# First attention of a two-layer encoder: exponentials divided where they stand, values of the last four heads made later

## The chip, the cores and the metric

The kernel runs on one core of one Trainium2 chip. The core has four engines that matter here, each working through its own instructions strictly in its own order: PE (TensorE, the matrix products, which write into eight banks of accumulator memory), DVE (VectorE), ACT (ScalarE) and POOL (GpSimd); SP starts most DMAs. [...] The metric is the device time of one execution in microseconds.

## The reference

Two encoder layers over 512 tokens of width 1024, in fp32. The first is a latent attention of 8 heads with a block-causal mask, and the change touches only that one:

```python
def block_attn(args):
    qn, qr, blk = args
    s = (jnp.einsum('bqhd,bkhd->bhqk', qn, k_nope) + jnp.einsum('bqhr,bkr->bhqk', qr, k_rope)) * scale
    mask = key_chunk[None, :] <= q_chunk[:, None]
    s = jnp.where(mask[None, None], s, -jnp.inf)
    p = jax.nn.softmax(s, axis=-1).astype(v.dtype)
    return jnp.einsum('bhqk,bkhd->bqhd', p, v)
```

Behind it come the output projection, a gated feed-forward block, a second attention with 16 heads over shared keys and values, and another feed-forward block.

## The kernel before

Every fp32 operand of a matrix product is split in two: a rounded part written by ACT (line 144, tiles whose names end in h or hi) and the rest written by DVE (line 145, names that end in l or lo). `mm3` (lines 355 to 358) then makes three products of them. Tiles are 128 partitions wide.

In the first attention, `Head.scores` handles one tile of 128 queries at a time: five products per tile into a bank `sc`, a DVE instruction that scales, masks and takes the minimum (line 494), an exponential on ACT that also sums its row into one column of `sums` (line 496). `Head.turn` transposes that tile on PE, piece by piece against an identity matrix, into a bank `pt` (line 508) and splits it into `pth` and `ptl`. `pv` multiplies with the values. The rows of the exponentials are not yet divided by their sums at that point: the result, whose columns are queries, has to be multiplied by the inverse sums, and for that each column of `sums` is spread over a bank `bc` by four PE transposes (`spread`, line 469):

```python
            V.reciprocal(sums, sums)
            of = U(name="of")
            nc.scalar.copy(of, o)

            def rest():
                V.tensor_tensor(of, of, spread(sums), op=OP.mult)
                oh, ol = U(F32R, "oh"), U(F32R, "ol")
                split(oh, ol, of)
```

`attention` goes through 32 slots, one for each of the 8 heads' 4 tiles of queries: the scores of a slot, the turn of the tile two slots back, and at the third slot of a head the `pv` of the head before. Between these it takes steps from a filler, a generator that yields after every projection product (`fill_a`). Its order is: values of heads 0 to 3 (`values_a(0)`), the query rotation of heads 0 to 3 (`rotary(0)`), head 0's queries and keys (`heads_a(0)`, 15 products of 512 columns), then `values_a(1)` (24 such products, the values of heads 4 to 7), then heads 1 to 7, with `rotary(1)` ahead of head 4, then the first part of the output projection. Thirteen steps are taken between head 0's projections and its first scores. The weights of all this come through one queue, `feed`, in the order in which they are used: raw tiles by DMA, then `whi` and `wlo` by ACT and DVE, three buffers of each.

The program's text gives priorities; a scheduler fixes the order on each engine ahead of the run. `first(n)` lifts the instructions within it by n places. Banks are handed out from three groups: four of `mm` (projections, `pv`), two of `s` (scores), two of `t` (transposes, `bc`). A projection's bank is free again when both its halves have been read out of it, by ACT and then by DVE.

Of the kernel before, what the change touches and what calls it, by code (L numbers as in the profile page):

```python
# [11 lines left out]
F32R = mybir.dt.float32r  # L12
I32 = mybir.dt.int32
AF = mybir.ActivationFunctionType
OP = mybir.AluOpType
# [3 lines left out]
D, S, P = 1024, 512, 128  # L19
KT = D // P  # L20
CHUNK = 64
H_A, NOPE, ROPE, VD = 8, 128, 64, 128
# [46 lines left out]
def trunk(ctx: ExitStack, tc: tile.TileContext, a, out):  # L69
    nc = tc.nc  # L70
    V = nc.vector
# [10 lines left out]
    def name_(n):  # L82
        uid[0] += 1
        return f"{n}_{uid[0]}"

    def U(dt=F32, name="u"):
        return up.tile([P, S], dt, tag="u", name=name_(name), bufs=NU)
# [4 lines left out]
    def bank(tag="mm", name="b"):  # L92
        return ps.tile([P, S], F32, tag=tag, name=name_(name), bufs={"mm": 4, "s": 2, "t": 2}[tag])

    def small(name="sm"):
        return sp.tile([P, 4], F32, tag="small", name=name_(name))
# [38 lines left out]
    @contextmanager  # L135
    def first(n):

        tc.cur_priority -= n
        yield
        tc.cur_priority += n  # L140


    def split(dst_hi, dst_lo, src):
        return (nc.scalar.copy(dst_hi, src),  # L144
                V.tensor_tensor(dst_lo, src, dst_hi.bitcast(F32), op=OP.subtract))  # L145
# [5 lines left out]
    class Pair:  # L151
# [4 lines left out]
        def __init__(self, src):  # L156
            self.src, self.raw = src, {}
# [191 lines left out]
    feed = Feed()  # L349
# [5 lines left out]
    def mm3(o, l, r, start, stop):  # L355
        nc.tensor.matmul(o, l[0], r[0], start=start, stop=False)  # L356
        nc.tensor.matmul(o, l[0], r[1], start=False, stop=False)  # L357
        nc.tensor.matmul(o, l[1], r[0], start=False, stop=stop)  # L358

    def proj(n_out, n_k, kc, rhs, banks, ahead=True):  # L360

        cols = n_out * P
        for c in range(0, n_k, kc):
            m = min(kc, n_k - c)
            w = feed.next(m * cols, ahead)
            for kk in range(m):
                if kk == 1:
                    feed.ahead()
                while len(rhs) <= c + kk:
                    yield False  # L370
                for j in range(n_out):
                    mm3(banks[j], w(kk * cols + j * P, P), rhs[c + kk], c + kk == 0, c + kk == n_k - 1)
                    yield True
# [9 lines left out]
    def cut(t, c):  # L383
        return t[0][:, c], t[1][:, c]
# [80 lines left out]
    def spread(col, first=0):  # L465

        b = bank("t", "bc")
        for i in range(col.shape[1]):
            nc.tensor.transpose(b[:, (first + i) * P:(first + i + 1) * P],
                                col[:, i:i + 1].to_broadcast([P, P]), ident)  # L470
        return b
# [8 lines left out]
    class Head:  # L480

        def __init__(self, qk, bt, scale, pv, sums):
            self.qk, self.bt, self.scale, self.pv, self.sums = qk, bt, scale, pv, sums
            self.p, self.pt = {}, None

        def scores(self, qt):
            n = P * (qt + 1)
            sc = bank("s", "sc")  # L490
            self.qk(sc[:, :n], qt, n)
            p = U(name="p")
            mn = small("mn")
            V.tensor_tensor_reduce(p[:, :n], sc[:, :n], self.bt(n), scale=self.scale(qt), scalar=3e38,  # L494
                                   op0=OP.add, op1=OP.min, accum_out=mn[:, :1])
            nc.scalar.activation(p[:, :n], p[:, :n], AF.Exp, bias=mn[:, :1], scale=-1.0,  # L496
                                 accum_out=self.sums[:, qt:qt + 1])
            self.p[qt] = p

        def turn(self, qt):  # L500
# [226 lines left out]
        feed.add(a["w_aq"][k], 768)  # L727
    feed.add(a["w_uv"][0], 1024)
    feed.add(a["w_uqr"][0], 768)
    feed.add(a["w_qk"][0], 640)  # L730
    feed.add(a["w_uv"][1], 1024)
    for h in range(1, H_A):
        if h == 4:
            feed.add(a["w_uqr"][1], 768)
        feed.add(a["w_qk"][h], 640)
# [50 lines left out]
    for k in range(KT):  # L786
        h, l = U(F32R, "xh"), U(F32R, "xl")
# [12 lines left out]
    rest = proj(3, KT, 2, xs, b2)  # L800
# [55 lines left out]
    for j in range(2):  # L856
        V.tensor_tensor(ckv[j], ckv[j], rkv, op=OP.mult)
        h, l = U(F32R, "ckh"), U(F32R, "ckl")
# [9 lines left out]
    for j in range(3):  # L868
        h, l = U(F32R, "cqh"), U(F32R, "cql")
        split_scaled(h, l, b2[j], g_q[:, j:j + 1])  # L870
        cqs.append((h, l))
    nsq = consts.tile([P, 4], F32, name="nsq")
# [6 lines left out]
    def A(name):  # L879
        return pool[0].tile([P, S], F32R, tag="a", name=name_(name), bufs=15)  # L880

    va = [pool[0].tile([P, 2, D], F32R, tag="v", name=f"va{tt}", bufs=4) for tt in range(NQT)]
    mask = pool[0].tile([P, S], F32, tag="mask", name="mask", bufs=1)
    nc.gpsimd.memset(mask, 0.0)
    nc.gpsimd.memset(mask[:64, S - 64:], -BIG)
    qr, qk_a, osp = {}, {}, []

    def values_a(c):

        w = feed.next(1024, False)  # L890
        for tt in range(NQT):
            if tt == 1:
                feed.ahead()
            b = bank()
            ts_ = slice(tt * P, (tt + 1) * P)
            for k in range(2):
                mm3(b, cut(cks[k], ts_), w(k * S, S), k == 0, k == 1)
                yield True
            with first(90 if c else 0):
                split(va[tt][:, 0, c * S:(c + 1) * S], va[tt][:, 1, c * S:(c + 1) * S], b)  # L900
# [23 lines left out]
    def heads_a(h):  # L924
        bq = bank()
        w = feed.next(640, False)
        for k in range(3):
            if k == 2:
                feed.ahead()
            mm3(bq, w(k * P, P), cqs[k], k == 0, k == 2)  # L930
            yield True
        qh, ql, kh, kl = (A(n) for n in ("qh", "ql", "kh", "kl"))
        split(qh, ql, bq)
        bk = bank()
        for k in range(2):
            mm3(bk, w((3 + k) * P, P), cks[k], k == 0, k == 1)
            yield True
        split(kh, kl, bk)
        qk_a[h] = qh, ql, kh, kl
        yield h  # L940
# [30 lines left out]
    def query_norm():  # L971
        for j in range(3):
            sq_.add(b2[j])
        rq = rstd_of_scaled(sq_.total(), QL, r0)
        V.tensor_scalar(nsq, rq, -((NOPE + ROPE) ** -0.5), None, op0=OP.mult)

    def rotary_key():

        nc.gpsimd.tensor_tensor(sik[:64], kr[64:], sik[64:], op=OP.mult)
        nc.gpsimd.tensor_tensor(kr[:64], kr[:64], cos[:64], op=OP.mult)  # L980
        nc.gpsimd.tensor_tensor(kr[:64], kr[:64], sik[:64], op=OP.add)
        for e in (LO, HI):
            nc.scalar.copy(kr1[e], kr[:64])
            V.tensor_tensor(kr2[e], kr[:64], kr1[:64].bitcast(F32), op=OP.subtract)

    def fill_a():
        yield from values_a(0)
        query_norm()
        yield from rotary(0)
        rotary_key()  # L990
        yield from heads_a(0)
        yield from values_a(1)
        yield "v"
        for h in range(1, H_A):
            if h == 4:
                yield from rotary(1)
            yield from heads_a(h)
        yield from out_first(osp)

    def start_a(h):  # L1000
        fill.until(h)
        qh, ql, kh, kl = qk_a.pop(h)
        r = qr.pop(h)

        def qk(o, qt, n):
            q_ = slice(qt * P, (qt + 1) * P)
            nc.tensor.matmul(o, qh[:, q_], kh[:, :n], start=True, stop=False)
            nc.tensor.matmul(o, qh[:, q_], kl[:, :n], start=False, stop=False)
            nc.tensor.matmul(o, ql[:, q_], kh[:, :n], start=False, stop=False)
            nc.tensor.matmul(o, r[:, q_], kr1[:, :n], start=False, stop=False)  # L1010
            nc.tensor.matmul(o, r[:, q_], kr2[:, :n], start=False, stop=True)

        def pv(pth, ptl):
            fill.until("v")
            o = bank()
            v_ = slice(h * VD, (h + 1) * VD)
            for kt in range(NQT):
                q_ = slice(kt * P, S)
                mm3(o[:, q_], (va[kt][:, 0, v_], va[kt][:, 1, v_]), (pth[:, kt, q_], ptl[:, kt, q_]),
                    kt == 0, kt == NQT - 1)  # L1020
            V.reciprocal(sums, sums)
            of = U(name="of")
            nc.scalar.copy(of, o)

            def rest():
                V.tensor_tensor(of, of, spread(sums), op=OP.mult)
                oh, ol = U(F32R, "oh"), U(F32R, "ol")
                split(oh, ol, of)
                osp.append((oh, ol))

            return rest

        sums = small("sums")
        return Head(qk, lambda n: mask[:, S - n:], lambda qt: nsq[:, qt:qt + 1], pv, sums)

    firsts = []
    fill = Filler(fill_a())
    attention(H_A, start_a, fill, 13, 8 + 5 * 7 + 6 + 14, False)
    fill.drain()
    st.close()  # L1040
# [462 lines left out]
    rest = v_half(0)  # L1503
# [11 lines left out]
    osp, qk_b, ofs, sums, biases = [], {}, {}, {}, {}  # L1515
# [116 lines left out]
    fill = Filler(fill_b())  # L1632
# [108 lines left out]
```

## Time and profile before

| what | us |
|---|---|
| median of 3 runs | 1124.07 (1122.27 to 1124.4) |
| the profiled execution's own time | 1122.24 |
| its span, first to last instruction | 1120.5 |
| first score product of head 0 | 65.7 from the span's start |
| inverse sums of head 0 and of head 7 taken | 75.2 and 148.3 |

Times within the profile are counted from the start of the span; the execution's own time is 1.7 us longer. A row of the timeline gives the start, the duration, the engine, the line and operation, output and input, shapes, and in square brackets how long the engine had nothing to do before it and what ended that. PEld is the loading of a product's stationary operand.

### The profile page before, as it was taken

The page shows a single profiled execution, that of the slowest core. Times are in us where ns is not written, and L with a number is a line of the kernel's source. Part 1 is how long each engine was busy: PE and PEld are TensorE (multiplying, and loading weights), DVE is VectorE, ACT ScalarE, POOL GpSimd, SP SyncE. Part 2 cuts the span into 40 slices and gives each one's busy share as a digit, 9 for nine tenths or more (in the row PEclk, how much of TensorE's full clock was granted, in tenths as well). Part 3 has the DMA queues.
Part 4 walks back from the last instruction along what each step waited for, and adds up shares of the span by engine and source line. Part 5 has one row for each costly group of instructions (what it writes and reads, how often), then busy time and mean ns, then how long its engine had stood idle before and what let it go on. Part 6 is the DMA issues. An engine that isn't in the chain of part 4 may idle for free.

```text
span 1120.5 us, 18982 instructions
## 1 busy us (share of the span) xinstructions
PE 1104.6 (99%) x6973; PEld 984.4 (88%) x6973; DVE 932.4 (83%) x1671; ACT 685.5 (61%) x1339; POOL 69.1 (6%) x106
## 2 busy tenths in 40 slices
PE   9999999999999999999999999999999999999997
PEld 6788889999999998887788888889999999998885
DVE  6787737999989889978868887758999899889977
ACT  6476636755555556768435767656755555566675
POOL 1200000000000001400000000000000000002402
PEclk9999999999999999999999999999999999999999
DMA  7342216323232358861556565635423322459923
GB/s 234 107 117 67 85 56 227 133 70 107 94 127 95 125 167 241 145 202 29 193 150 168 142 178 148 165 103 181 148 78 95 125 84 95 142 169 289 172 57 76
DMA packets 62990, 150.85 MB, mean 135 GB/s; under 512 B 8432, under 2 KB 10224, under 8 KB 62896
## 3 DMA queue, kind: packets, MB, share of 16 engines
q1 hardware_dynamic: 55552, 136.61, 38.7%
q0 software_dynamic: 6912, 12.59, 6.8%
q8 instruction: 55, 0.90, 0.3%
q10 hardware_dynamic: 432, 0.44, 0.1%
q14 instruction: 39, 0.32, 0.1%
HBM read 119.52 MB, written 9.63 MB: 115 GB/s over the span
## 4 chain that ended last, share of the span: by engine, by line
PE 46%; DVE 3%; DMA 2%; issue 1%; ACT 1%; POOL 0%; SPq 0%; POOLq 0%; DVEq 0%; ACTq 0%
PE al L1446 8%; PE b L356 6%; PE b L357 6%; PE b L358 6%; PE be L1446 4%; PE al L1197 4%; PE be L1197 3%; PE ga L1446 2%; PE pt L508 1%; PE de L1197 1%; PE ga L1197 1%; PE b L1600 1%; PE b L1599 1%; PE sc L1592 1%; PE sc L1591 1%
## 5 line engine op out<-in xcount | busy, mean ns | idle before, releaser
L144 ACT CAST whi<-raw 128x1024 fp32r<-128x1024 f32 (+3 forms) x224 | 225.5, 1007 | 212.6 <-PE al L1446 73.0
L145 DVE TENSOR_TENSOR wlo<-raw,whi 128x1024 fp32r<-128x1024 f32 (+3 forms) x224 | 261.3, 1168 | 57.7 <-ACT whi L144 54.3
L1446 PE MATMUL al<-th,whi 128*128 128x256 f32 x432 | 123.0, 285 | 0.4 <-DVE ut L1458 0.3
L1446 PE MATMUL al<-th,wlo 128*128 128x256 f32 x432 | 121.2, 281 | 0.0
L1446 PE MATMUL al<-tl,whi 128*128 128x256 f32 x432 | 121.0, 280 | 0.0
L356 PE MATMUL b<-xh,whi 128*128 128x512 f32 (+1 forms) x304 | 117.6, 387 | 0.1
L357 PE MATMUL b<-xl,whi 128*128 128x512 f32 (+1 forms) x304 | 113.0, 372 | 0.1
L358 PE MATMUL b<-xh,wlo 128*128 128x512 f32 (+1 forms) x304 | 112.4, 370 | 0.3 <-DVE wlo L145 0.3
L174 DVE TENSOR_TENSOR raw<-raw,raw 128x1024 f32<-128x1024 f32 x72 | 86.7, 1220 | 1.2 <-DMA raw<-in_w_pair 0.9
L1446 PEld LDWEIGHTS al<-th,whi 128*128 128x128 f32 x432 | 81.3, 188 | 2.9 <-DVE ut L1458 0.8
L1446 PEld LDWEIGHTS al<-th,wlo 128*128 128x128 f32 x432 | 81.3, 188 | 0.4 <-DVE wlo L145 0.4
L1446 PEld LDWEIGHTS al<-tl,whi 128*128 128x128 f32 x432 | 81.3, 188 | 0.0
L496 ACT ACTIVATE p<-p,mn 128x128 f32<-128x128 f32 (+1 forms) x96 | 54.0, 563 | 39.5 <-DVE mn L494 38.4
L145 DVE TENSOR_TENSOR ptl<-pt,pth 128x128 fp32r<-128x128 f32 (+1 forms) x96 | 46.7, 487 | 29.4 <-ACT pth L144 23.7
L358 PEld LDWEIGHTS b<-xh,wlo 128*128 128x128 f32 x304 | 57.5, 189 | 10.1 <-DVE wlo L145 0.7
L144 ACT CAST whi<-wd 128x512 fp32r<-128x512 f32 x86 | 49.9, 620 | 26.8 <-PE al L1197 11.9
L145 DVE TENSOR_TENSOR wlo<-wd,whi 128x512 fp32r<-128x512 f32 x86 | 56.5, 689 | 11.5 <-ACT whi L144 11.2
L356 PEld LDWEIGHTS b<-xh,whi 128*128 128x128 f32 x304 | 57.7, 190 | 7.5 <-ACT xh L148 1.0
L357 PEld LDWEIGHTS b<-xl,whi 128*128 128x128 f32 x304 | 57.7, 190 | 7.3 <-DVE xl L149 1.4
L144 ACT CAST pth<-pt 128x128 fp32r<-128x128 f32 (+1 forms) x96 | 40.4, 421 | 26.6 <-PE pt L508 25.6
L1197 PE MATMUL al<-whi,ph 128*128 128x512 f32 x132 | 51.9, 393 | 0.5 <-ACT y L1258 0.5
L1197 PE MATMUL al<-whi,pl 128*128 128x512 f32 x132 | 51.5, 391 | 0.0
(309 smaller groups left out, 3267.4 us busy)
## 6 DMA issues: line engine op xcount, KB each, us to landing
raw<-in_w_pair SPq DMA_DIRECT2D x72, 512.0 KB, 3.6
wd<-in_w_down SPq DMA_DIRECT2D x54, 256.0 KB, 5.6
raw<-in_w_o SPq DMA_DIRECT2D x16, 512.0 KB, 3.5
raw<-in_w_gu SPq DMA_DIRECT2D x16, 512.0 KB, 3.8
raw<-in_w_down SPq DMA_DIRECT2D x16, 512.0 KB, 4.1
raw<-in_w_qkb SPq DMA_DIRECT2D x16, 512.0 KB, 3.5
wd<-in_w_down POOLq DMA_DIRECT2D x22, 256.0 KB, 5.6
wd<-raw POOLq DMA_DIRECT2D x22, 256.0 KB, 4.2
```

The source lines that it names most:

```text
L144: return (nc.scalar.copy(dst_hi, src), V.tensor_tensor(dst_lo, src, dst_hi.bitcast(F32), op=OP.subtract))
L145: V.tensor_tensor(dst_lo, src, dst_hi.bitcast(F32), op=OP.subtract))
L174: V.tensor_tensor(t, x, y, op=OP.add)
L356: nc.tensor.matmul(o, l[0], r[0], start=start, stop=False)
L357: nc.tensor.matmul(o, l[0], r[1], start=False, stop=False)
L358: nc.tensor.matmul(o, l[1], r[0], start=False, stop=stop)
L496: nc.scalar.activation(p[:, :n], p[:, :n], AF.Exp, bias=mn[:, :1], scale=-1.0, accum_out=self.sums[:, qt:qt + 1])
L508: nc.tensor.transpose(t[:, kt * P:(kt + 1) * P], p[:, kt * P:(kt + 1) * P], ident)
L1197: nc.tensor.matmul(to[e], l[c], r[d], start=j < 4 and k == 0 and n == 0, stop=k == NF // 2 - 1 and n == 2, skip_group_check=True)
L1446: nc.tensor.matmul(o, l[c], r[d], start=first_ and n == 0, stop=k == K2 - 1 and n == 2, skip_group_check=True)
L1591: nc.tensor.matmul(o, q1[:, e, q_], k1[:, e, :n], start=True, stop=False)
L1592: nc.tensor.matmul(o, q1[:, e, q_], k2[:, e, :n], start=False, stop=True)
```

## The change

The first attention's heads pass a new flag, `whole`. With it, `scores` divides a tile of exponentials by its sums as soon as they are there: an inverse of one column and a multiplication of the tile by it, both on DVE, both lifted by 20 places. `pv` then splits its bank directly into `oh` and `ol`; the copy `of`, the spreading of the sums and the multiplication with them are gone. In the filler, `values_a(1)` and the mark "v" move from behind head 0 to ahead of head 3, its weights move likewise in `feed`, and only heads 4 to 7 wait for "v".

```diff
+            if self.whole:
+                r = self.sums[:, qt:qt + 1]
+                with first(20):
+                    V.reciprocal(r, r)
+                    V.tensor_scalar(p[:, :n], p[:, :n], r, None, op0=OP.mult)
             self.p[qt] = p
...
-    feed.add(a["w_qk"][0], 640)
-    feed.add(a["w_uv"][1], 1024)
-    for h in range(1, H_A):
+    for h in range(H_A):
+        if h == 3:
+            feed.add(a["w_uv"][1], 1024)
         if h == 4:
...
-        yield from heads_a(0)
-        yield from values_a(1)
-        yield "v"
-        for h in range(1, H_A):
+        for h in range(H_A):
+            if h == 3:
+                yield from values_a(1)
+                yield "v"
             if h == 4:
...
         def pv(pth, ptl):
-            fill.until("v")
+            if h >= 4:
+                fill.until("v")
...
-            V.reciprocal(sums, sums)
-            of = U(name="of")
-            nc.scalar.copy(of, o)
-
-            def rest():
-                V.tensor_tensor(of, of, spread(sums), op=OP.mult)
-                oh, ol = U(F32R, "oh"), U(F32R, "ol")
-                split(oh, ol, of)
-                osp.append((oh, ol))
-
-            return rest
+            oh, ol = U(F32R, "oh"), U(F32R, "ol")
+            split(oh, ol, o)
+            return lambda: osp.append((oh, ol))
...
-        return Head(qk, lambda n: mask[:, S - n:], lambda qt: nsq[:, qt:qt + 1], pv, sums)
+        return Head(qk, lambda n: mask[:, S - n:], lambda qt: nsq[:, qt:qt + 1], pv, sums, True)
```

The line numbers of the changed kernel are 5 higher from line 498 up to `pv`. Three places show how the order on the engines moves. The first is PE behind head 0's projections, whose banks are b_688 (queries) and b_710 (keys). Before, the next rows there were the values (whi_697 here is their weight, ckh the latent keys), each bank of which is read out on its own. The first bank's six rows are shown; the first score product stood 36 rows behind b_710:

```order
L358 MATMUL b_710<-ckh_465,wlo_628 128x512
L356 MATMUL b_720<-whi_697,ckh_460 128x512
L357 MATMUL b_720<-wlo_698,ckh_460 128x512
L358 MATMUL b_720<-whi_697,ckl_461 128x512
L356 MATMUL b_720<-whi_697,ckh_465 128x512
L357 MATMUL b_720<-wlo_698,ckh_465 128x512
L358 MATMUL b_720<-whi_697,ckl_466 128x512
...
L1007 MATMUL sc_788<-kh_706,qh_704 128x128
```

In the changed kernel the same place on PE holds head 1's queries (b_720) and keys (b_742), the first score product after 15 rows, and then head 2's queries (b_751), the fifth bank in a row of a group of four:

```order
L358 MATMUL b_710<-ckh_465,wlo_628 128x512
L356 MATMUL b_720<-cqh_525,whi_697 128x512
...
L358 MATMUL b_742<-ckh_460,wlo_698 128x512
L356 MATMUL b_742<-ckh_465,whi_697 128x512
L357 MATMUL b_742<-ckl_466,whi_697 128x512
L358 MATMUL b_742<-ckh_465,wlo_698 128x512
L1012 MATMUL sc_786<-kh_706,qh_704 128x128
L356 MATMUL b_751<-cqh_525,whi_729 128x512
```

So 21 rows of projections have moved from ahead of the first score product to behind it. The second place is ACT just ahead of the splits of head 0's banks (qh_704 and kh_706). Before, with rh the rotated queries, kr_117 the rotated key, va the values:

```order
L144 CAST whi_771<-raw_695 128x640
L144 CAST rh_648<-ra_643 128x512
L144 CAST va_543<-b_720 128x512
L144 CAST va_544<-b_735 128x512
L144 CAST va_545<-b_744 128x512
L144 CAST rh_657<-ra_652 128x512
L144 CAST qh_704<-b_688 128x512
L144 CAST va_546<-b_753 128x512
L983 CAST kr_117_538<-kr_469 64x512 x2
L144 CAST kh_706<-b_710 128x512
L144 CAST whi_838<-raw_729 128x640
```

and in the changed kernel:

```order
L144 CAST whi_760<-raw_695 128x1024
L144 CAST rh_648<-ra_643 128x512
L144 CAST whi_805<-raw_727 128x640
L144 CAST rh_657<-ra_652 128x512
L988 CAST kr_117_538<-kr_469 64x512 x2
L144 CAST qh_704<-b_688 128x512
L144 CAST kh_706<-b_710 128x512
L144 CAST qh_736<-b_720 128x512
```

Here four casts of values have left, the cast of a further weight (whi_805, head 3's) has come ahead of rh_657, and the key's rotation has come ahead of qh_704. The third place is DVE in the same stretch. Before:

```order
L145 TENSOR_TENSOR wlo_772<-raw_695,whi_771 128x640
L145 TENSOR_TENSOR rl_649<-ra_643,rh_648 128x512
...
L911 TENSOR_TENSOR ra_652<-ra_652,rb_653 128x512
L145 TENSOR_TENSOR va_545<-b_744,va_545 128x512
L145 TENSOR_TENSOR rl_658<-ra_652,rh_657 128x512
L145 TENSOR_TENSOR ql_705<-b_688,qh_704 128x512
L145 TENSOR_TENSOR va_546<-b_753,va_546 128x512
L984 TENSOR_TENSOR kr_118_539<-kr_469,kr_117_538 64x512 x2
L145 TENSOR_TENSOR kl_707<-b_710,kh_706 128x512
```

and in the changed kernel:

```order
L145 TENSOR_TENSOR wlo_761<-raw_695,whi_760 128x1024
L145 TENSOR_TENSOR rl_649<-ra_643,rh_648 128x512
L914 TENSOR_TENSOR ra_652<-b_617,sin_406 128x512
L915 TENSOR_TENSOR rb_653<-b_618,cos_407 128x512
L145 TENSOR_TENSOR wlo_806<-raw_727,whi_805 128x640
L916 TENSOR_TENSOR ra_652<-ra_652,rb_653 128x512
L145 TENSOR_TENSOR rl_658<-ra_652,rh_657 128x512
L989 TENSOR_TENSOR kr_118_539<-kr_469,kr_117_538 64x512 x2
L145 TENSOR_TENSOR ql_705<-b_688,qh_704 128x512
L145 TENSOR_TENSOR kl_707<-b_710,kh_706 128x512
```

The split ql_705, with which head 0's query bank comes free, now stands behind the low half of head 3's weight (wlo_806) and behind both halves of the rotated key. From a place within the output projection on, the order is the same as before on every engine, apart from the numbers.

More of the change, by code (lines that the diff above doesn't have):

```diff
@@ L480, in trunk, with __init__ @@
     class Head:
-        def __init__(self, qk, bt, scale, pv, sums):
-            self.qk, self.bt, self.scale, self.pv, self.sums = qk, bt, scale, pv, sums
+        def __init__(self, qk, bt, scale, pv, sums, whole=False):
+            self.qk, self.bt, self.scale, self.pv, self.sums, self.whole = qk, bt, scale, pv, sums, whole
             self.p, self.pt = {}, None
```

## The prediction

> **What bounds the kernel now.** I read the page first (busy time by engine), then the windows of the first attention, then the list of who waited for whom there.
>
> ```profile
> span 1120.5 us, 18982 instructions
> PE 1104.6 (99%) x6973; PEld 984.4 (88%) x6973; DVE 932.4 (83%) x1671; ACT 685.5 (61%) x1339; POOL 69.1 (6%) x106
> ```
>
> ```profile
> 60.00:80.00 20.00, 19.87 (x107) 16.83 (x106) 17.22 (x38) 15.63 (x35) 0.00 (x0) 1.00 0.48 134
> 80.00:100.00 20.00, 19.77 (x119) 17.08 (x118) 14.06 (x34) 11.49 (x29) 0.00 (x0) 1.00 0.10 30
> 100.00:120.00 20.00, 19.64 (x116) 16.82 (x117) 16.69 (x41) 13.91 (x35) 0.00 (x0) 1.00 0.44 130
> 120.00:140.00 20.00, 20.00 (x121) 17.74 (x120) 14.89 (x35) 13.44 (x34) 0.00 (x0) 1.00 0.16 52
> ```
>
> ```profile
> PEld b L356 <- DVE va L145: 1.1, 2, 0.6
> PEld sc L1007 <- DVE mn L494: 0.8, 2, 0.4
> ```
>
> In a window's row stand its length, then PE, PEld, DVE, ACT and POOL, then the granted clock and the DMA. The reader is to see that PE has something to do nearly all the time, in this stage too, at full clock. The longest waits for others between 58 and 172 us (in the last two rows: total, times, longest) come to no more than a microsecond or so. So a microsecond of PE work removed is worth about a microsecond, and an idle microsecond added to PE costs one: behind it PE is full to the end, and nothing makes it up. DVE has 5.9, 3.3 and 5.1 us free in the three windows from 80 to 140.
>
> **What leaves PE.** Eight heads lose one spreading of the sums each:
>
> ```profile
> 82.12 0.60 PE L469 MATMUL bc<-ident,sums 128*128 128x128 f32 x4
> 82.56 0.38 PE L508 MATMUL pt<-ident,p 128*128 128x128 f32 x2
> 165.09 0.62 PE L469 MATMUL bc<-ident,sums 128*128 128x128 f32 x4
> 165.46 0.36 PE L356 MATMUL b<-oh,whi 128*128 128x256 f32 x1
> ```
>
> Durations overlap, so starts count: 0.44 us of PE for the first, 0.37 for the last. Eight times that is 3.0 to 3.5; I take **3.4 us off**, since most stand within the loop like the first.
>
> **What DVE and ACT gain and lose.** The groups of instructions by line give count, busy time, mean ns of one, and the idle time ahead of them:
>
> ```profile
> L1023 ACT COPY of<-b 128x512 f32<-128x512 f32 x8 | 4.7, 585 | 5.8 <-PE b L358 5.8
> L1026 DVE TENSOR_TENSOR of<-of,bc 128x512 f32<-128x512 f32 x8 | 5.5, 682 | 3.0 <-ACT of L1023 2.6 <-PE bc L469 0.4
> L1021 DVE RECIPROCAL sums<-sums 128x4 f32<-128x4 f32 x8 | 1.4, 176 | 1.2 <-ACT p L496 0.9
> L817 DVE TENSOR_SCALAR rot<-rot,inv 128x128 f32<-128x128 f32 x1 | 0.3, 285 | 0.0
> L1368 DVE TENSOR_SCALAR g<-g 128x512 f32<-128x512 f32 x1 | 0.4, 419 | 0.0
> ```
>
> Per head DVE gets four inverses of one column (no such row; with 0.176 for four columns as a ceiling, 0.7 together) and multiplications of 128, 256, 384 and 512 columns. With 0.285 and 0.419 as their ends and the others between, those are 1.4 us; at the 0.68 of a product with a second tensor per 512 columns they would be at most 1.9. It loses 0.68 + 0.18. So DVE gains 1.2 to 1.7 us a head, and nearly six heads fall into 80 to 140, which had 14.4 us free: 7 to 10 of those would be used. That stays beside PE, at about 90%. It costs nothing while the splits still come in time, and the first places where they may not are below. ACT loses 4.7 us, hidden before and after. The longer chain from a tile's scores to its transposes (some 0.5 us more) lies within the two slots, about 5 us, that PE works in between.
>
> **What the move costs.** Here the order printed ahead of this text decides. In the changed kernel PE does 15 rows behind head 0's banks, and then the first score product needs `kh` of head 0 from ACT, and the next row needs a bank, which only head 0's `ql` on DVE frees: queries and keys of heads 0 and 1 fill all four. Before, 36 rows lay there, with value banks that came free one by one. What the timeline of before says of those two splits, PE first, then ACT, then DVE:
>
> ```profile
> 56.68 0.39 PE L356 MATMUL b<-whi,ckh 128*128 128x512 f32 x1
> 56.91 0.39 PE L357 MATMUL b<-wlo,ckh 128*128 128x512 f32 x1
> 65.69 0.22 PE L1007 MATMUL sc<-kh,qh 128*128 128x128 f32 x1
> ```
>
> ```profile
> 56.70 0.73 ACT L144 CAST whi<-raw 128x640 fp32r<-128x640 f32 x1 [3.16 <-PE b L357]
> 57.33 0.62 ACT L144 CAST rh<-ra 128x512 fp32r<-128x512 f32 x1
> 62.58 0.58 ACT L144 CAST qh<-b 128x512 fp32r<-128x512 f32 x1
> 63.65 1.26 ACT L983 CAST kr<-kr 64x512 fp32r<-64x512 f32 x2
> 64.92 0.59 ACT L144 CAST kh<-b 128x512 fp32r<-128x512 f32 x1
> ```
>
> ```profile
> 57.46 0.83 DVE L145 TENSOR_TENSOR wlo<-raw,whi 128x640 fp32r<-128x640 f32 x1 [0.57 <-ACT whi L144]
> 58.20 0.16 DVE L462 TENSOR_TENSOR r<-r,r 128x4 f32<-128x4 f32 x1
> 62.71 0.69 DVE L145 TENSOR_TENSOR rl<-ra,rh 128x512 fp32r<-128x512 f32 x1
> 63.32 0.69 DVE L145 TENSOR_TENSOR ql<-b,qh 128x512 fp32r<-128x512 f32 x1
> 64.52 1.38 DVE L984 TENSOR_TENSOR kr<-kr,kr 64x512 fp32r<-64x512 f32 x2
> L145 DVE TENSOR_TENSOR wlo<-raw,whi 128x1024 fp32r<-128x1024 f32 x198 | 241.8, 1222 | 49.9 <-ACT whi L144 47.3 <-DMA raw<-in_w_down 2.1
> ```
>
> The row at 56.68 is the first behind b_710, and product follows product every 0.227 us, so the 15 rows end at 56.68 + 3.4 = 60.1. DVE meanwhile, queued behind the inverse root at 58.2: `nsq` to 58.4, the low half of the value weight (1.14 from start to start at this size) to 59.5, `rl`, `ra`, `rb` at 0.60 each to 61.3, the low half of head 3's weight (0.74) to 62.0, the last `ra` with its 0.68 to 62.7. ACT's `rh` can only then run, to 63.4; then `kr` 1.26 to 64.6, `qh` to 65.1, `kh` to 65.6. So the first score product stands at about 65.65 instead of 60.1. DVE's `kr` waits for ACT's and ends at 65.4, `ql` at 66.0, so the next row stands at 66.05. PE is idle for some **5.9 us**. The lower end takes the casts of whi_805 to be all that gates (its buffer is free when row 14 ends, at 60.0): `wlo` to 61.7, `ra` 62.3, `rh` 62.9, `kr` 64.1, `qh` and `kh` 65.2, `ql` 65.6: 5.4. Nothing covers it, as PE takes its rows in order.
>
> Against this, the kernel before reached the first score product at 65.69 with 21 more rows done (21 x 0.227 = 4.8), and its two waits for value splits (1.1 in PEld's row above, 0.6 as pitch) lie within that. The changed one is at the same place 4.5 to 5.0 us later: **4.9 us**.
>
> **Two small waits behind it.** In head 0 DVE has the late `kl` of head 2 and a value split ahead of the fourth tile's line 494 (2 x 0.6, an inverse 0.17, 0.67, the third tile's multiplication 0.35: 2.4 us from the end of the scores), where PE has 2.1 us of rows until it needs that tile. Some 0.5 us is late there, and as much at head 0's `pv`, whose `ptl` now stands behind a weight split. From nothing to 2, I take **1 us**.
>
> **The clock.** The windows and the timeline show no pause of PE of this length, except at the ends:
>
> ```profile
> 1112.60:1116.00 3.40, 0.52 (x3) 0.10 (x1) 2.49 (x6) 0.72 (x2) 1.00 (x1) 1.00 0.21 77
> 1116.00:1120.50 4.50, 0.00 (x0) 0.00 (x0) 1.46 (x3) 0.00 (x0) 0.00 (x0) 0.51 0.49 175
> 1.19 4.02 PE L113 MATMUL warm<-idle 128*128 128x512 bf16 x9 [1.19 <-DVE idle L110]
> 6.69 0.42 PE L358 MATMUL b<-xh,wlo 128*128 128x512 f32 x1
> ```
>
> Some 3 us after the last product the granted clock is at half (0.51), and at the start products of 512 columns stand 0.43 to 0.45 apart (4.02 for nine) until about 6.7, 5.5 us after the first. An idle stretch of 5.9 us is longer than 3, so the clock falls; then PE runs at half for up to 5.5 us, which loses up to half of that, 2.75. I take **1.4 us**, the middle of 0 and 2.75. [...]
>
> **The sum.** -3.4 + 4.9 + 1.0 + 1.4 = +3.9 us on the profiled execution's 1122.24 (1120.5 of span): 1126.1. The median of the runs shown lies 1.8 above that execution, so on it the same sum gives 1128.0. I predict **1127.0**, between the two.
>
> **Rivals.**
> - *The move is harmless* (faster). ACT and DVE reach head 0's splits by 60.1, since four value splits on each (ACT 0.59, DVE 0.60) have left. Then -3.4, and the 0.6 of the value waits goes as well, +1 for the small waits: 1119.2 on the profiled execution. For it: in before, `qh` was ready at 63.2, not 65. Against it: the rotated key, and `rh` behind a weight whose buffer PE frees at 60.0. It decides if `ql` ends before 61.5.
> - *About even.* The idle stretch is there, but no clock loss, no small waits, and the pauses PE makes later in this stage (0.8 for line 494 above) vanish with the relieved banks: -3.4 + 4.9 - 0.8 = +0.7: 1122.9, or 1124.8 on the median.
> - *DVE becomes the bound.* At 90% over heads 1 to 5, with each inverse waiting for ACT, PE waits a further 0.8 us a head: 3.9 + 4 = 1130.1. Against it: DVE's rows sum to less than PE's in each of those heads except that with the second rotation (six more products of 0.6).
>
> That the change does not do what it says is out: the printed order has no line 469 on `sums`, and the values stand behind head 2.
>
> **Chances.** Forecast (+2.3 to +6) 0.50, about even 0.25, DVE the bound 0.13, harmless 0.12. A measurement can tell about 0.2%, 2.25 us. Faster by more: 0.12. Within: the even case and a little of the forecast, 0.27. Slower: 0.61. The range leaves out the harmless case and the far end of DVE's: 1121.5 to 1131. The likeliest case's own is 1124.5 to 1130.
>
> **What would show it.** In the profile after: a pause of PE of 5 to 6 us between 60 and 66, ended by ACT `kh` and DVE `ql`; a granted clock under 1.00 in the windows behind it; no line 469 rows on `sums`; multiplications of 0.2 to 0.45 us; the end of the stage 3 to 5 us later. If PE's first score product comes at 61 or 62, the move is harmless and I am wrong on the whole. If the pause is there and the clock stays at 1.00, the sum is 1.4 less. If DVE's rows between 80 and 120 fill 19 of 20 us and PE waits for `ptl` in each head, it is the third rival.

## The result, and the profile after

| | before | after |
|---|---|---|
| median of 5 runs each | 1122.27 us (1120.22 to 1124.4) | 1130.52 us (1129.52 to 1132.24) |
| ratio, 95% interval | | 1.0079 [1.0066, 1.0091] |
| profiled execution: time, span | 1122.24, 1120.5 | 1132.24, 1130.5 |

The changed kernel is slower by 8 us, where the forecast was 4. The profiled execution of the changed kernel is the slowest of its five, 1.7 us over the median; its span is 10.0 us longer than that of before. The head of its page, and four windows of the first attention (length, then PE, PEld, DVE, ACT and POOL, then the granted clock and the DMA):

```profile
span 1130.5 us, 18959 instructions
PE 1106.1 (98%) x6941; PEld 986.1 (87%) x6941; DVE 940.4 (83%) x1719; ACT 681.4 (60%) x1331; POOL 69.1 (6%) x106
```

```profile
60.00:80.00 20.00, 14.99 (x59) 12.09 (x58) 12.93 (x28) 11.22 (x22) 0.00 (x0) 0.83 0.38 108
80.00:100.00 20.00, 20.00 (x120) 17.71 (x119) 16.65 (x51) 11.93 (x32) 0.00 (x0) 1.00 0.17 54
100.00:120.00 20.00, 17.66 (x96) 14.11 (x95) 17.87 (x43) 11.96 (x27) 0.00 (x0) 0.99 0.38 98
120.00:140.00 20.00, 20.00 (x113) 17.81 (x113) 16.32 (x53) 12.22 (x33) 0.00 (x0) 0.93 0.17 62
```

PE has 32 rows fewer, as it should (6941 for 6973). It is idle in two windows, not in one: 5 us between 60 and 80, and 2.3 between 100 and 120, with a full one in between. The clock falls twice. The list of waits from 56 to 190 us (total, times, longest) has both behind one name, and a smaller one in the output projection, where the first total (`tot`) waits for DVE's sum of squares:

```profile
PEld sc L1012 <- ACT kh L144: 7.3, 2, 5.4
PEld tot L435 <- DVE acc L426: 0.9, 1, 0.9
```

The first pause is the forecast one. In the timeline, PE's last row of head 1's keys starts at 59.84 and the first score product at 65.22; ACT's `kh` and DVE's `ql` of head 0, for which it and the next row wait, start at 64.57 and 64.96:

```profile
59.84 0.39 PE L358 MATMUL b<-ckh,wlo 128*128 128x512 f32 x1
65.22 0.48 PE L1012 MATMUL sc<-kh,qh 128*128 128x128 f32 x1 [4.99 <-ACT kh L144]
65.71 0.80 PE L356 MATMUL b<-cqh,whi 128*128 128x512 f32 x1
```

```profile
64.57 0.59 ACT L144 CAST kh<-b 128x512 fp32r<-128x512 f32 x1
```

```profile
64.96 0.69 DVE L145 TENSOR_TENSOR ql<-b,qh 128x512 fp32r<-128x512 f32 x1
```

The second was not in the forecast's sum. It lies where head 3 ends and head 4 begins. PE first, then ACT:

```profile
114.58 0.48 PE L357 MATMUL b<-ckl,whi 128*128 128x512 f32 x1
114.90 0.40 PE L358 MATMUL b<-ckh,wlo 128*128 128x512 f32 x1
115.54 0.63 PE L513 MATMUL pt<-ident,p 128*128 128x128 f32 x4 [0.25 <-DVE p L502]
117.80 0.49 PE L1012 MATMUL sc<-kh,qh 128*128 128x128 f32 x2 [1.63 <-ACT kh L144]
```

```profile
115.24 1.05 ACT L144 CAST whi<-raw 128x1024 fp32r<-128x1024 f32 x1
116.18 0.59 ACT L144 CAST qh<-b 128x512 fp32r<-128x512 f32 x1
116.66 0.60 ACT L144 CAST pth<-pt 128x512 fp32r<-128x512 f32 x1
117.14 0.61 ACT L144 CAST kh<-b 128x512 fp32r<-128x512 f32 x1
```

Behind head 3's last transposes PE has nothing but head 4's scores, and those wait for a `kh` that stands on ACT behind the first output weight (1.05 us), `qh` and `pth`. The same place in the kernel before:

```profile
107.68 0.60 PE L508 MATMUL pt<-ident,p 128*128 128x128 f32 x4
108.03 0.48 PE L356 MATMUL b<-ckh,whi 128*128 128x512 f32 x1
...
109.51 0.40 PE L356 MATMUL b<-pth,va 128*128 128x512 f32 x1
109.74 0.39 PE L1007 MATMUL sc<-kh,qh 128*128 128x128 f32 x2
```

There six rows of head 5's keys and one of `pv` lay behind the transposes. In the changed kernel those six stand ahead of them, because the transposes now come later: they wait for the multiplication.

The clock behind both pauses, in windows of 3.41 us cut where it changes (the first row is 3.96 us long):

```profile
61.00:64.96 3.96, 0.00 (x0) 0.00 (x0) 3.23 (x5) 2.62 (x5) 0.00 (x0) 1.00 0.37 86
64.96:68.38 3.42, 3.15 (x7) 2.44 (x8) 2.49 (x4) 1.19 (x3) 0.00 (x0) 0.50 0.46 107
68.38:71.79 3.41, 3.41 (x9) 2.65 (x8) 0.69 (x1) 0.59 (x1) 0.00 (x0) 0.50 0.59 165
71.79:75.20 3.41, 3.41 (x21) 2.93 (x20) 1.23 (x3) 3.10 (x6) 0.00 (x0) 1.00 0.32 103
116.17:119.58 3.41, 1.69 (x11) 1.27 (x10) 3.26 (x5) 2.55 (x6) 0.00 (x0) 1.00 0.55 138
119.58:122.99 3.41, 3.41 (x13) 3.22 (x12) 2.24 (x9) 1.09 (x4) 0.00 (x0) 0.50 0.61 246
122.99:126.40 3.41, 3.41 (x23) 3.02 (x23) 3.03 (x11) 1.96 (x6) 0.00 (x0) 1.00 0.01 2
```

The new rows on DVE are as cheap as forecast (count, busy time, mean ns of one, idle time ahead):

```profile
L501 DVE RECIPROCAL sums<-sums 128x1 f32<-128x1 f32 x32 | 5.1, 160 | 6.1 <-ACT p L496 6.0
L502 DVE TENSOR_SCALAR p<-p,sums 128x512 f32<-128x512 f32 x8 | 3.9, 487 | 0.2
L502 DVE TENSOR_SCALAR p<-p,sums 128x384 f32<-128x384 f32 x8 | 3.3, 418 | 0.1
L502 DVE TENSOR_SCALAR p<-p,sums 128x256 f32<-128x256 f32 x8 | 2.8, 354 | 0.2
L502 DVE TENSOR_SCALAR p<-p,sums 128x128 f32<-128x128 f32 x8 | 2.3, 284 | 0.1
```

To see where the 10.0 us lie, I added up, over all PE rows of a trace, by how much the next row starts later than the pitch of its size (the median from start to start in the changed kernel's trace: 0.227 us for 512 columns, 0.175 for 384, 0.118 for 256, 0.108 for 128). This is PE's **lost time**, in us by stretches of the span:

| | 0 to 50 | 50 to 100 | 100 to 150 | 150 to 200 | behind 200 |
|---|---|---|---|---|---|
| before | 5.61 | 1.93 | 1.80 | 0.99 | 18.44 |
| after | 5.62 | 8.88 | 5.76 | 1.52 | 20.43 |
| difference | 0.0 | +6.95 | +3.96 | +0.53 | +1.99 |

The differences sum to 13.4; less 32 transposes at 0.108 (3.5), that is the 10.0, to a tenth. Of the first 6.95, 2.6 are 13 rows at half clock (66.3 to 71.8); of the 3.96, 1.6 are the 24 rows from 119 to 124.

### The profile page after: what moved, and what is told of

The parts are those of the page before. It is cut to its first block, busy times and chain, and to the rows that moved or that the text cites. A ratio compares the mean times of both kernels' runs of the same rounds, so it can differ in the third digit from the quotient of the medians.

```text
span 1130.5 us, 18959 instructions
## 1 busy us (share of the span) xinstructions
PE 1106.1 (98%) x6941; PEld 986.1 (87%) x6941; DVE 940.4 (83%) x1719; ACT 681.4 (60%) x1331; POOL 69.1 (6%) x106
## 4 chain that ended last, share of the span: by engine, by line
PE 47%; DVE 2%; DMA 2%; issue 1%; ACT 1%; POOL 0%; POOLq 0%; SPq 0%; DVEq 0%; ACTq 0%
PE al L1444 9%; PE b L356 5%; PE b L358 5%; PE b L357 5%; PE be L1444 5%; PE al L1195 4%; PE be L1195 3%; PE ga L1444 2%; PE pt L513 1%; PE de L1195 1%; PE ga L1195 1%; DMA raw<-in_w_gu 1%; DMA raw<-in_w_qkb 1%; PE b L1598 1%; PE b L1597 1%
```

## The experiments

All have 5 rounds beside the kernel before on the same chip; ratios are to that.

**One part alone.** Theory A: the division keeps what it takes off PE, and the whole loss is the move's. Theory B: the division gives it back at head 4. The first run has only the division (the parts of the diff on `Head` and `pv`), the second only the later values (the parts on `feed`, `fill_a` and `fill.until`), with the old way of dividing. The third is the changed kernel with work that nobody reads put into the first pause:

```diff
     def start_a(h):
         fill.until(h)
+        if h == 1:
+            wb = bank("t", "warm")
+            for _ in range(20):
+                nc.tensor.matmul(wb, cks[0][0][:, :P], cks[0][0], start=True, stop=True)
```

> Computes the reference; the exponentials are divided where they stand, the values of heads 4 to 7 stand where they stood before. Theory A (the whole loss comes from the move: PE pauses 5.4 us on head 0's splits, the clock falls, and head 4's first scores come late behind it): no pause of PE over 1 us between 55 and 125, granted clock 1.00 there, 3 to 4 us less than before (ratio 0.9965 to 0.9975). Theory B (DVE's added work makes head 4 late whatever stands ahead): a pause of 1 to 3 us at head 4, ended by ACT or DVE, which takes back the 3.5 us or more: ratio 0.9990 to 1.002.

> Computes the reference; the heads' outputs are divided as before (sums spread by PE), the values of heads 4 to 7 stand ahead of head 3. Theory A: the same first pause of 5.4 us, granted clock at half for 3.4 to 6.8 us behind it, and the pause at head 4 too: 10 to 12 us over before (ratio 1.009 to 1.011). Theory B: the first pause and its clock, but none at head 4, since DVE has its old load: 6.5 to 8.5 us over before (ratio 1.006 to 1.0075).

> The changed kernel with 20 further products of 128x512 into a bank that nobody reads, behind head 1's projections, where PE pauses; the reference is computed. They take 20 x 0.227 = 4.5 us of the 5.4 us pause and hold up nothing, since PE waits there for ACT. If the clock's fall is a cost of its own: granted clock 1.00 from 60 to 80, the time 2.5 to 3.5 us below the changed kernel's (ratio to before 1.0045 to 1.006). If the time lost is only the wait for ACT's and DVE's splits: as the changed kernel, ratio 1.007 to 1.009.

| run | median us | ratio [95%] | 50 to 100 | 100 to 150 | 150 to 200 | behind 200 |
|---|---|---|---|---|---|---|
| kernel before, same chip | 1121.54 | | | | | |
| division alone | 1122.23 | 1.0003 [0.9994, 1.0011] | 1.81 | 5.50 | 1.91 | 20.26 |
| move alone | 1128.27 | 1.0058 [1.0046, 1.0070] | 8.28 | 2.38 | 1.15 | 16.74 |
| changed, first pause filled | 1127.48 | 1.0049 [1.0035, 1.0064] | 1.61 | 5.76 | 2.35 | 20.42 |

(The last columns are the lost time.) It is B, with the move's ratio just under what B expected. The two stretches belong to one part each. The move makes the first pause, and costs 6.5 us by itself. The division takes 3.5 us off PE and gains nothing, because it makes the second pause. In its list of waits and its windows:

```profile
PEld sc L1012 <- ACT kh L144: 1.9, 1, 1.9
PEld tot L435 <- DVE acc L426: 1.3, 1, 1.3
```

```profile
106.01:109.42 3.41, 1.53 (x9) 0.78 (x8) 2.99 (x6) 3.39 (x7) 0.00 (x0) 1.00 0.46 107
109.42:112.83 3.41, 3.41 (x13) 2.90 (x13) 3.36 (x10) 1.17 (x4) 0.00 (x0) 0.50 0.84 305
112.83:116.24 3.41, 3.41 (x24) 3.14 (x22) 2.02 (x7) 1.75 (x6) 0.00 (x0) 1.00 0.02 5
```

The filled pause gives 0.0030 back (3.4 us, give or take 2 by the two intervals), though the 20 products take 4.5 us of PE and only fill its wait. What it took away is the half clock behind it (granted clock 1.00 from 60 to 80 us, where the changed kernel has 0.83): that is a cost by itself.

**Why the division is late at head 4.** Two theories: the order (O), or DVE's extra load (D). The split queries and keys of a head lie in a pool of 15 tiles (`A`); given tiles from the general pool (`U`), head 4's casts move on ACT from behind the 1024-column weight to ahead of those of head 3's last two transposed tiles. The runs are the division alone with that edit, the kernel before with that edit and the new DVE instructions writing to a tile that nobody reads (where the text has them, not lifted), the changed kernel with that edit and the filled pause, and the kernel before with that edit.

```diff
-        qh, ql, kh, kl = (A(n) for n in ("qh", "ql", "kh", "kl"))
+        qh, ql, kh, kl = (U(F32R, n) if h == 4 else A(n) for n in ("qh", "ql", "kh", "kl"))
```

```diff
+            if self.bt(P) is not None and junk: V.reciprocal(junk[0][:, :1], self.sums[:, qt:qt + 1]); V.tensor_scalar(junk[0][:, :n], p[:, :n], junk[0][:, :1], None, op0=OP.mult)
             self.p[qt] = p
```

> Division alone, values at their old place, and head 4's four query and key tiles from the general pool. Theory O (the division loses its gain at one joint: its later transposes let the products for head 5 run ahead of them, nothing is left in front of head 4's scores, and the splits of head 4's queries and keys, which wait for tiles of a full pool, stand behind a 128x1024 weight cast on ACT): no pause on kh between 104 and 114, clock 1.00 there, ratio to the kernel before 0.9965 to 0.9985, 3 us under the division alone. Theory D (DVE's extra 1.2 us a head makes everything late that DVE prepares, whatever the order): pauses of the same sum elsewhere, ratio 0.9992 to 1.0015.

> The kernel before with the same reciprocals and multiplications on DVE, written to a tile that nobody reads (the sums are still spread and multiplied as before, so nothing of PE's work goes), and head 4's four tiles from the general pool. Theory O (order, not load): 0.9995 to 1.0015, no pause over 0.6 us in the stage. Theory D (load): what the division gave back is due to these instructions alone, 3 to 4 us: ratio 1.0025 to 1.0035.

> The changed kernel with 20 products that nobody reads in its first pause, and head 4's four tiles from the general pool. Theory O: the second pause and its fall of the clock go, 3 us under the kernel with the first pause filled (ratio 1.0049): 1.0015 to 1.0028, clock 1.00 in every window from 60 to 180. Theory D: 1.004 to 1.0055.

> The kernel before with head 4's four tiles from the general pool and nothing else. Theory O: there is no pause at that place to remove, ratio 0.9988 to 1.0010, the same as the kernel before. Rival (own tiles are worth something whatever the division does, so that the run of the division with own tiles proves nothing): 0.996 to 0.998.

| run | median us | ratio [95%] | 50 to 100 | 100 to 150 | 150 to 200 | behind 200 |
|---|---|---|---|---|---|---|
| kernel before, same chip | 1120.31 | | | | | |
| division, own tiles | 1119.69 | 0.9999 [0.9989, 1.0009] | 1.83 | 2.71 | 1.93 | 19.06 |
| load, own tiles | 1120.77 | 1.0007 [0.9998, 1.0016] | 2.06 | 2.30 | 1.08 | 18.05 |
| changed, filled, own tiles | 1122.64 | 1.0019 [1.0010, 1.0029] | 1.61 | 2.82 | 1.41 | 17.49 |
| before, own tiles | 1119.96 | 0.9999 [0.9991, 1.0008] | 2.03 | 2.04 | 0.96 | 17.46 |

With own tiles for head 4, DVE's load alone costs 0.8 us [0.2 gained, 1.8 lost], not the 3 to 4 that D asked for; own tiles alone are worth nothing. (No tile waits for these instructions, so the run prices their time on DVE and not a later tile.) In the changed kernel they take off 0.0030, as O said. For the division alone O's number was missed: the wait on `kh` and the half clock are gone (granted clock 1.00 from 100 to 120 us, 0.91 without own tiles), but a shorter pause has come in their place (a row of PE's timeline, and a window around it):

```profile
108.74 0.63 PE L513 MATMUL pt<-ident,p 128*128 128x128 f32 x4 [1.05 <-DVE p L502]
```

```profile
106.00:109.40 3.40, 2.35 (x19) 1.94 (x18) 2.89 (x8) 3.39 (x8) 0.00 (x0) 1.00 0.46 102
```

The multiplication for head 3's last tile now stood on DVE behind a split of head 5's queries.

**Following the pause.** Own tiles for head 5 too (`if h in (4, 5)`) put the multiplication ahead of that split. The second run also holds back the weight splits in the output projection until the squares for its first total are done, and the third also the first output weight's, until head 5's keys are split (`feed.behind[i]` orders a weight's split behind an instruction). The fourth is the third with the multiplication on ACT.

```diff
-                nc.scalar.activation(q[:, c], src, AF.Square)
+                self.last = nc.scalar.activation(q[:, c], src, AF.Square)
...
-                self.half(h, KT - len(banks), banks)
+                self.half(h, KT - len(banks), banks); feed.behind.setdefault(len(feed.ready) + 0, (self.sum.last,) if len(feed.ready) < 60 else ())
...
-        split(kh, kl, bk)
+        feed.behind[24 if h == 5 else -1] = split(kh, kl, bk)
...
-                    V.tensor_scalar(p[:, :n], p[:, :n], r, None, op0=OP.mult)
+                    nc.scalar.activation(p[:, :n], p[:, :n], AF.Copy, scale=r)
```

> Division alone with own tiles for heads 4 and 5: head 5's query split no longer stands on DVE ahead of the multiplication that head 3's last transposes wait for. Theory O (each loss is a place in the order, and can be taken away): the 1.2 us pause of the run before goes down to under 0.4, the stage ends 2.3 to 2.7 us ahead of the kernel before, ratio 0.9975 to 0.9988. Rival (the time saved in the stage is taken up again further on): pause gone in the same way, ratio 0.9993 to 1.0005.

> The same, and in the output projection the two splits of 128x1024 weights on ACT and DVE stand behind the squares that the first total waits for. Theory O: the 1.3 us wait of the total on DVE's sum falls to under 0.5, ratio 0.8 us lower than the run without it: 0.9968 to 0.9982. Rival (time taken up again further on, by the weight splits that are now later): 0.999 to 1.0005, with new waits for weights behind 180 us.

> The last kernel (division alone, own tiles for heads 4 and 5, sums first), and the split of the first 128x1024 output weight on ACT and DVE stands behind head 5's keys, out of the joint from head 3 to head 4. Theory O: the 1.2 us pause on line 494 between 105 and 112 falls under 0.4 and the stage ends 3.0 to 3.5 us ahead of the kernel before; ratio 0.9968 to 0.9985. Rival (taken up again behind the stage, where PE waits for weights of the second attention at 600 to 650 us): stage the same 3.0 to 3.5 ahead, ratio 0.9990 to 1.0003.

> The same with the multiplication by the inverse on ACT (copy with a scale) in place of DVE, so DVE has 10 us less in the stage and ACT 14 us more. If DVE's load still costs something there: 0.5 to 1 us under the run with it on DVE. If order is all: the same within 0.0005. If ACT's later casts cost more: 1 to 3 us over it, with waits of PE on ACT kh, pth or p.

| run | median us (before, same chip) | ratio [95%] | 50 to 100 | 100 to 150 | 150 to 200 | behind 200 |
|---|---|---|---|---|---|---|
| own tiles, heads 4 and 5 | 1121.03 (1121.48) | 1.0000 [0.9989, 1.0010] | 1.79 | 3.22 | 2.22 | 19.20 |
| and sums first | 1120.86 (1121.48) | 0.9999 [0.9990, 1.0008] | 1.76 | 3.27 | 0.81 | 19.87 |
| and weight behind | 1119.15 (1121.01) | **0.9978 [0.9970, 0.9987]** | 1.76 | 2.40 | 0.85 | 20.34 |
| and multiplication on ACT | 1119.81 (1121.01) | 0.9987 [0.9978, 0.9996] | 1.98 | 2.79 | 0.81 | 20.80 |

The first two ratios lie in their rivals' range, the third in O's. In the first of these the pause moved a second time. On DVE the multiplication is in time, then 1.23 us of weight stand ahead of line 494, for which PE waits. DVE's rows, then PE's, then a window with the pause:

```profile
107.74 0.49 DVE L502 TENSOR_SCALAR p<-p,sums 128x512 f32<-128x512 f32 x1
108.47 1.23 DVE L145 TENSOR_TENSOR wlo<-raw,whi 128x1024 fp32r<-128x1024 f32 x1 [0.25 <-DMA qr<-rh]
109.61 0.35 DVE L494 CUSTOM_DVE_ANT_0 p<-sc,mask,nsq 128x128 f32<-128x128 f32 x1
```

```profile
110.02 0.44 PE L1012 MATMUL sc<-kh,qh 128*128 128x384 f32 x1 [1.02 <-DVE mn L494]
```

```profile
107.50:110.90 3.40, 2.20 (x15) 1.79 (x15) 3.08 (x9) 2.42 (x7) 0.00 (x0) 1.00 0.49 106
```

With the weight out of the joint no pause above 0.55 us is left, and the division with the three edits is worth 2.5 us [1.5, 3.4]: this kernel is faster than the kernel before and the changed one. So order **and** room count: at this joint DVE has the splits of heads 4 and 5, head 3's transposes and a weight to do, and with the weight held back the multiplications fit in. Elsewhere they fit as they are. Not run were the weight's new place without the other two edits, and all three edits with the old way of dividing. For the second the trace speaks against a gain of the edits by themselves: from 50 to 200 us this kernel loses 5.01 us and the kernel before 4.72, so what it is ahead by is the 3.5 us of rows that left PE. On ACT they gain nothing more: that run lies between the same and a small loss, 0.0009 higher with intervals that overlap.

"Sums first" did its part in the trace (150 to 200: 2.22 to 0.81), and the measured time did not follow. In that execution the stage ended 2.3 us ahead of before (lost time from 50 to 190 us 1.1 more, less 3.5), and the runs show 0.1 us [1.1 faster, 0.9 slower]. Own tiles for head 4 alone had the same gap, 1.7 us ahead at 200 us by the trace and 0.1 by the runs. That stays open, as does what the last column shows: behind 200 us the order of instructions is the same in all, yet before and the three runs that divide the old way lost 16.7 to 18.4 us there, nine of the ten with the new way 19.1 to 20.8, and one 17.5 (the last run, below, is counted in). These are single executions, but the 2.1 us that the ten lost more there on average than the four would be about enough for such gaps. Part of it lies in the second attention, where DVE waits for weights to land. From 590 to 650 us, before and then after:

```profile
DVE raw L306 <- DMA raw<-in_w_qkb: 1.4, 1, 1.4
```

```profile
DVE raw L306 <- DMA raw<-in_w_qkb: 5.4, 4, 2.5
```

What makes these waits longer was not tried.

**The move with the division mended.** The last run is the changed kernel with the three edits of the fastest.

> The changed kernel (division and the later values) with the three edits of the fastest kernel: own tiles for heads 4 and 5, the first output weight's split behind head 5's keys, sums first. What is left over against that kernel (ratio 0.9978) is the move of the values alone. Theory P (division and move do not act on each other: the move costs what it cost with the old division, 1.0058, whatever comes later): ratio 1.0028 to 1.0048, a pause of 5 to 5.5 us on kh at 60 to 66 with the clock at half for two windows behind it, no other pause above 0.6 us. Theory Q (with the values behind head 2 the stage has less room, so the joint at head 4 is late again): 1.006 to 1.008.

Measured: 1125.07 us (before 1119.75), ratio 1.0050 [1.0037, 1.0064]; lost time 8.91, 2.49, 0.86 and 19.71. By the trace it is P: the first pause stands as it was, nothing above 0.55 us behind it.

```profile
57.79 0.39 PE L358 MATMUL b<-ckh,wlo 128*128 128x512 f32 x1
63.17 0.47 PE L1012 MATMUL sc<-kh,qh 128*128 128x128 f32 x1 [4.99 <-ACT kh L144]
```

```profile
62.42:65.84 3.42, 2.65 (x6) 2.08 (x7) 2.95 (x5) 1.68 (x4) 0.00 (x0) 0.56 0.41 96
65.84:69.25 3.41, 3.41 (x9) 2.64 (x9) 0.69 (x1) 0.58 (x1) 0.00 (x0) 0.50 0.53 137
```

The ratio lies just above P's range and its interval reaches into both. Beside the move the mended division is worth 0.9 us by the ratios (1.0058 less 1.0050), give or take 2; behind 200 us this run loses 19.71 where the move alone lost 16.74.

## Why the prediction went wrong in size

The direction and the range held; the forecast move (+3.9 us) was less than half of what came. That the range held is in part luck: its upper end was made for the third rival (1130.1), and the time came there by another way. By the trace's 10.0 us, the terms came as -3.5 for -3.4, 4.4 for 4.9, nothing for 1.0 and 2.6 for 1.4, and three came that the sum did not have: 4.0 at the second pause, 0.5 in the output projection (most of it the wait for the first total) and 2.0 behind 200 us, which no run explains.

- **What leaves PE**, 3.4 us: right, 32 rows at 0.108 are 3.5.
- **The first pause**, 5.9 us, net 4.9: right. PE stood from 59.84 to 65.22 and lost 0.75 us more at the next two rows, 5.9 together; without the clock the stretch costs 6.95 - 2.6 = 4.4 net. The move alone, forecast at 4.9 + 1.0 + 1.4 = 7.3, measured 6.5 [5.2, 7.9].
- **Two small waits in head 0**, 1 us: not there. From 72 to 100 us all rows together lose 0.4 us.
- **The clock**, 1.4 us: mis-sized. It was "the middle of 0 and 2.75", though the prediction's own rows had products of 512 columns 0.43 to 0.45 us apart at the start, and at half clock (0.50, 64.96 to 71.79 us) those of the changed kernel are 0.43 apart; two windows of it cost 2.6, and the unforeseen second fall 1.6. Filling the pause gave a price by itself of 3.4 us, from ratios of two sets of runs.
- **DVE's gain**: this is the step that failed. "That stays beside PE, at about 90%. It costs nothing while the splits still come in time, and the first places where they may not are below": the durations were right, and the places below were all in head 0. The place that mattered was the joint of heads 3 and 4. The third rival was set aside because "DVE's rows sum to less than PE's in each of those heads except that with the second rotation", and that exception lies right ahead of the place: the second rotation's six products start between 102.1 and 108.0 us, and DVE was busy for 17.87 of the 20 us from 100 to 120. The rival itself did not come true: PE waited for `kh` at one joint and not for `ptl` in each head. I had counted 14.4 us of free DVE time over three windows, and what decided were 3 us of one of them. It cost 4.0 us with its clock, and the division's 3.5 were gone.
- What would show it: the pause, its two releasers, the clock under 1.00 and the missing line 469 rows came as listed, and the multiplications but for the longest (0.49 for 0.45). "The end of the stage 3 to 5 us later" did not: the first total of the output projection starts at 189.86 us instead of 182.58, 7.3 later.

On the second fall of the clock: PE was busy for 1.69, 1.53 and 1.91 of 3.41 us in the windows ahead of the fall (changed kernel, division alone, first pause filled), never wholly idle. The forecast took the clock to fall because the idle stretch was longer than 3 us; in the changed kernel it fell behind a pause of 1.8 us too, and that cost 1.6 us. The prediction had a sign of this in its own rows: PE was busy for 0.52 us of the window from 1112.60 to 1116.00, and the clock was at half behind that one too.

## What to carry to other kernels

Work that moves onto an engine with free time is not free because a window of 20 us has room: look at each joint where the bottleneck engine has no cover, and at what stands there ahead of the instruction it waits for. The changed kernel's two long pauses had two prices each, their length and the clock behind them: the second was 1.6 us behind the pause of 1.8 and 2.6 us behind the one of 5.2. Where a scheduler sets the order, a small edit can spend its gain at one place; look for that place before the edit is given up, since here moving one weight's split turned no gain into 2.5 us.

## What was unexpected of the hardware

- The clock fell although PE had been busy for half of the window before: 1.53, 1.69 and 1.91 us of 3.41. Busy time alone does not tell when. In the changed kernel the clock changed at 64.96, 71.79, 119.58, 122.99 and 1126.51 us, which is 2, 14, 1 and 294 times 3.413 us apart. Of the windows of that length laid from the fall in one run (first pause filled, 116.37 us), two have the same 1.91 us, and the clock fell behind the first and not behind the second:

```profile
112.96:116.37 3.41, 1.91 (x11) 1.50 (x12) 3.41 (x5) 2.33 (x5) 0.00 (x0) 1.00 0.81 223
771.72:775.13 3.41, 1.91 (x17) 1.71 (x16) 1.98 (x3) 3.27 (x6) 0.00 (x0) 1.00 0.18 72
```

  In the changed kernel the products that start in the window ahead of the second fall (116.17 to 119.58) have 1920 columns together; from 774.94 to 778.35, where PE was busy for 2.03 us and the clock stayed at 1.00 behind it, they have 3584. What decides was not shown: no run varied it.
- Behind the pauses it came back only after a window in which PE worked throughout (3.41 of 3.41 us). After windows with 3.15 (changed kernel), 3.06 (the last run, 62.83 to 66.25) and 1.64 us (move alone) it stayed at half for one more; after the short pauses one full window was enough.
- Multiplying by a column, DVE took 0.28 us for 128 columns and 0.07 more for each further 128, to 0.49 for 512, where a product with a second tensor takes 0.68.
